# The split operands of the down projection, in longer tiles and at 28 different starting words

## The chip, the core and the metric

The kernel runs on one NeuronCore of one Trainium2 chip. A core has five engines that run side by side, each with its own instruction stream: TensorE (PE, with its weight loads shown apart as PEld), VectorE (DVE), ScalarE (ACT), GpSimd (POOL) and SyncE (SP), which here only issues DMAs. They work on SBUF, an on-chip memory of 128 partitions, and TensorE writes its sums into PSUM, a second memory. The metric is the time of one execution on the device in microseconds; of the kernel before there are three runs, and their median counts.

## The reference

One decoder block in float32 on `x` of 1 x 1024 x 1024: a pooling mixer and a sliding-window attention are merged through sigmoid gates and added to `x`, and then comes the MLP, on whose second half this case turns:

```
    h2 = _rmsnorm(x, g_mlp_pre[l])
    ff = jnp.einsum('bsf,fd->bsd',
                    jnp.square(jax.nn.relu(jnp.einsum('bsd,df->bsf', h2, w_up[l]))), w_down[l])
    x = x + _rmsnorm(ff, g_mlp_post[l])
```

`w_up` is 1024 x 4096 and `w_down` 4096 x 1024. The second product, of the squared activations (1024 x 4096) and `w_down`, is the down projection.

## The kernel before

**Products in split float32.** Every large product is made of three matmuls in the type float32r (`F32R`). A float32 operand is split by `split` into `hi` (a cast on ACT, line 101) and `lo` = source minus `hi` (a subtraction on DVE, line 104), and the product is the sum hi x hi + hi x lo + lo x hi, which is what the table `PASSES` lists.

**Seven products in place of eight.** The gates, the up projection and the down projection each cut both matrices in 2 x 2 blocks and use seven block products of sums and differences of blocks (a Strassen-like scheme). For the down projection the up projection has stored the needed sums of its activations in `f_dram`; the differences of the blocks B11, B12, B21, B22 of `w_dn` are made on DVE in `operands` (lines 1245 to 1259).

**The down projection (to line 1360).** The seven products run in the order `PRODUCTS = (1, 5, 2, 3, 6, 7, 4)`. Each has `NS` = 8 steps, so there are 56 steps `(i, s_)` in one list. A step covers 256 rows of the contraction. `operands(i, s_)` brings a step's two source tiles by DMA (lines 1222, 1227 and 1236), makes the difference of weights where one is needed, and splits both: the activations `ft` into two tiles of the pool `wp`, tag "wh" (six slots), the weights `wt` into two tiles of the pool `ga_`, tag "ga" (six slots too). Then `down_mm` issues the 24 matmuls of the step: two blocks of 128 rows, four tiles `t` of 128 output rows, three passes. The activations are the stationary operand, loaded anew for each matmul (128 x 128); the weights are the moving operand, 512 columns.

Everything is written out in the order in which it is issued: at step `j` stands first `operands` of step `j + AHEAD` with `AHEAD` = 2, then the matmuls of step `j`. Six slots of two tiles a step hold the operands of three steps. The operands of step (1, 0) are made earlier, during the up projection, in other tiles (lines 1181 to 1190); the loop and the line before it call `operands` for the other 55 steps. Each product adds up in four PSUM tiles, tag "at" or "mm"; at its end these are copied or added into SBUF tiles. The last three steps of the last product (i = 4) are taken tile by tile: 18 matmuls finish one `t`, and then DVE and ACT do that tile's closing work (lines 1276 to 1346) while TensorE does the next.

**Where the tiles lie.** A tile has the same byte address in each partition. The slots of "wh" and "ga" are 4096 bytes long (2 x 512 float32). In the program as built, every slot that holds an operand of a large matmul, in these pools and in the others, begins 32 bytes past a multiple of 64, and within a slot the matmuls' operands begin at multiples of 512 bytes.

Of the kernel before, what the change touches and what calls it, by code (L numbers as in the profile page):

```python
# [9 lines left out]
F32R = mybir.dt.float32r  # L10
# [4 lines left out]
P = 128  # L15
# [35 lines left out]
def block_kernel(ctx: ExitStack, tc, xt, x, consts, vecs, sinks, b_qkv, g_post, g_mlp, g_mlp_post,  # L51
# [7 lines left out]
    wp = ctx.enter_context(tc.tile_pool(name="wp", bufs=6))  # L59
# [8 lines left out]
    def nm(s):  # L68
        cnt[0] += 1
        return f"{s}_{cnt[0]}"  # L70
# [4 lines left out]
    def wslot(shape):  # L75
        return wp.tile([P] + shape, F32R, tag="wh", name=nm("wh"))
# [3 lines left out]
    ga_ = ctx.enter_context(tc.tile_pool(name="ga", bufs=6))  # L80
# [18 lines left out]
    def split(hi, lo, src, eng=dve, first=None):  # L99
        if first is None:  # L100
            act.copy(hi, src)  # L101
        else:
            first.tensor_copy(hi, src)
        eng.tensor_tensor(lo, src, f32(hi), ALU.subtract)  # L104
# [435 lines left out]
    def ar(shape):  # L540
        return ga_.tile([P] + shape, F32R, tag="ga", name=nm("ar"))
# [268 lines left out]
    def gr(shape):  # L810
        return gp.tile([P] + shape, F32R, tag="g", name=nm("gr"))
# [61 lines left out]
    for p in range(8):  # L873
# [8 lines left out]
        tag = "at" if p % 2 == 0 else "mm"  # L882
# [248 lines left out]
    def f_block(c, s_):  # L1131
        return f_rows[s_, c]
# [41 lines left out]
    for p in range(1, NP):  # L1174
# [3 lines left out]
        tag = "at" if p % 2 == 0 else "mm"  # L1178
        if p == NP - 1:
# [6 lines left out]
            fo = wslot([2, 512]), wslot([2, 512])  # L1186
            split(*fo, early_raw[0][0])
            wo_ = gr([2, 512]), gr([2, 512])
# [23 lines left out]
    def raw_tile():  # L1212
        return dl.tile([P, 2, 512], F32, tag="raw", name=nm("raw"), bufs=4)
# [2 lines left out]
    rr = sp.tile([P, NT], F32, tag="frr", name="frr", bufs=1)  # L1216
    junk = dl.tile([P, 512], F32, tag="junk", name="junk", bufs=1)
    res, xf = {}, {}

    def resident(name, s_):  # L1220
        t = rp.tile([P, 2, 512], F32, tag="w", name=nm(name))
        nc.sync.dma_start(t, w_block(name, s_))
        res[name, s_] = t

    def streamed(name, s_):
        t = raw_tile()
        nc.sync.dma_start(t, w_block(name, s_))
        return t

    def operands(i, s_):  # L1230

        if i == 1 and s_ in early_raw:
            ft, wt = early_raw[s_]
        else:
            ft = raw_tile()
            nc.sync.dma_start(ft, f_block(A_OF[i], s_))
            if i == 1:
                resident("B11", s_)
                if s_ - 3 in early_raw:
                    resident("B11", s_ - 3)  # L1240
                wt = res["B11", s_]
            elif i == 5:
                resident("B12", s_)
                wt = res["B11", s_]
                dve.tensor_tensor(wt, res["B12", s_], wt, ALU.subtract)
            elif i == 2:
                wt = streamed("B21", s_)
            elif i == 3:
                resident("B22", s_)
                wt = res["B22", s_]  # L1250
            elif i == 6:
                wt = res["B11", s_]
                dve.tensor_tensor(wt, res["B22", s_], wt, ALU.subtract)
            elif i == 7:
                wt = res["B12", s_]
                dve.tensor_tensor(wt, res["B22", s_], wt, ALU.subtract)
            else:
                wt = streamed("B21", s_)
                dve.tensor_tensor(wt, wt, res["B11", s_], ALU.subtract)
        fo = wslot([2, 512]), wslot([2, 512])  # L1260
        split(*fo, ft)
        wo_ = ar([2, 512]), ar([2, 512])
        split(*wo_, wt)
        opers[i, s_] = fo, wo_

# [43 lines left out]
    for j in range(1, AHEAD):  # L1309
        operands(*steps[j])  # L1310
    for j, (i, s_) in enumerate(steps):
        if j + AHEAD < len(steps):
            operands(*steps[j + AHEAD])
        if s_ == 0 and i not in (2, 3):
            tag = "mm" if i in (5, 7) else "at"
# [117 lines left out]
```

## Time and profile before

| what | us |
|---|---|
| median of three runs (lowest, highest) | 1133.97 (1133.69, 1134.46) |
| the profiled execution, its own time | 1134.51 |
| its span in the profile | 1132.7 |
| PE busy in the span | 1114.8 (98%), 5183 matmuls |
| PE weight loads busy | 920.9 (81%) |
| DVE busy | 820.6 (72%) |
| ACT busy | 526.7 (47%) |
| POOL busy | 77.8 (7%) |

The span goes from the first to the last instruction of the program; 1.8 us of the profiled execution lie around it. A group's row gives line, engine, operation, the tiles it writes and reads (out<-in, buffer numbers left out), shapes and count, then busy time, the mean length of one in ns, and the idle time before them with what ended it. The chain is the work that ended last, followed back from the last instruction; its rows give start, length and what it was. A matmul's row is longer than its turn on TensorE, because matmuls overlap: how fast they follow each other is read from the chain, where a row's length divided by its count is the turn of one. The down projection is line 1270.

### The profile page before, as it was taken

The numbers are of one execution on the slowest core, as the hardware profiler recorded it, in microseconds if no ns is written. First come the engines' busy times: TensorE is split into PE (matmuls) and PEld (weight loads), VectorE is DVE, ScalarE is ACT, GpSimd is POOL, SyncE is SP. The second block draws the span as 40 slices with busy tenths as digits, with TensorE's granted clock in tenths as the row PEclk, the third lists the DMA queues.
The fourth block names the chain that finished last, engine by engine and source line by source line (L and its number), as shares of the span: only waits on it lengthen the run. The fifth ranks groups of instructions, "written<-read, shape, count | busy, mean of one in ns | idle before, by whom it ended". The sixth has DMA issues, their size and how long they took to land.

```text
span 1132.7 us, 14023 instructions
## 1 busy us (share of the span) xinstructions
PE 1114.8 (98%) x5183; PEld 920.9 (81%) x5183; DVE 820.6 (72%) x1210; ACT 526.7 (47%) x912; POOL 77.8 (7%) x111
## 2 busy tenths in 40 slices
PE   8999999999999999999999999999999999999997
PEld 7888778888888888888788888888888888888885
DVE  7668857899858885678998666666457955446787
ACT  6445655544432333446555444444444345344342
POOL 2443211000000330000000000000000000000000
PEclk9999999999999999999999999999999999999999
DMA  7205669366664444243365343434597765332652
GB/s 248 84 1 110 151 138 285 117 224 220 211 236 141 143 158 154 94 149 112 121 230 202 145 160 141 164 139 167 214 337 266 242 203 189 110 93 75 215 192 94
DMA packets 80179, 189.02 MB, mean 167 GB/s; under 512 B 6896, under 2 KB 19312, under 8 KB 80112
## 3 DMA queue, kind: packets, MB, share of 16 engines
q1 hardware_dynamic: 70144, 166.38, 43.8%
q10 hardware_dynamic: 5616, 19.66, 4.5%
q0 software_dynamic: 4352, 2.10, 1.8%
q8 instruction: 40, 0.66, 0.2%
q14 instruction: 27, 0.22, 0.1%
HBM read 132.54 MB, written 55.57 MB: 166 GB/s over the span
## 4 chain that ended last, share of the span: by engine, by line
PE 87%; DVE 7%; ACT 3%; DMA 2%; issue 1%; SPq 0%; DVEq 0%; ACTq 0%
PE mm L484 22%; PE at L484 16%; PE at L1270 14%; PE mm L1270 12%; PE mm L987 6%; PE mm L421 5%; PE mm L183 3%; PE mm L423 3%; PE mm L574 2%; PE at L987 1%; PE at L192 1%; DVE wh L104 1%; PE at L392 1%; PE sc L328 1%; DMA st<-in_w_up_dram 1%
## 5 line engine op out<-in xcount | busy, mean ns | idle before, releaser
L1270 PE MATMUL at<-ar,wh 128*128 128x512 f32 x744 | 169.6, 389 | 0.0
L1270 PEld LDWEIGHTS at<-ar,wh 128*128 128x128 f32 x744 | 139.6, 188 | 29.3 <-DVE ar L104 0.4
L1270 PE MATMUL mm<-ar,wh 128*128 128x512 f32 x576 | 131.0, 389 | 0.0
L1270 PEld LDWEIGHTS mm<-ar,wh 128*128 128x128 f32 x576 | 108.1, 188 | 22.5
L104 DVE TENSOR_TENSOR wh<-raw,wh 128x1024 fp32r<-128x1024 f32 x53 | 64.8, 1223 | 83.4 <-ACT wh L101 83.4
L101 ACT CAST wh<-raw 128x1024 fp32r<-128x1024 f32 x53 | 55.8, 1053 | 133.9 <-PE at L1270 60.3
L101 ACT CAST wh<-st 128x512 fp32r<-128x512 f32 (+1 forms) x105 | 66.3, 642 | 84.6 <-PE at L484 29.9
L104 DVE TENSOR_TENSOR wh<-st,wh 128x512 fp32r<-128x512 f32 (+1 forms) x105 | 81.8, 789 | 29.6 <-ACT wh L101 27.1
L484 PE MATMUL mm<-gr,wh 128*128 128x512 f32 x309 | 74.2, 390 | 0.0
L484 PE MATMUL mm<-T,wx 128*128 128x512 f32 x288 | 67.6, 389 | 0.0
L484 PEld LDWEIGHTS mm<-gr,wh 128*128 128x128 f32 x309 | 57.8, 188 | 11.8
L484 PEld LDWEIGHTS mm<-T,wx 128*128 128x128 f32 x288 | 54.1, 188 | 11.2
L484 PE MATMUL at<-T,wx 128*128 128x512 f32 x252 | 59.1, 389 | 0.0
L484 PEld LDWEIGHTS at<-T,wx 128*128 128x128 f32 x252 | 47.3, 188 | 9.8
L484 PE MATMUL mm<-x,wh 128*128 128x512 f32 x240 | 55.2, 389 | 0.0
L484 PEld LDWEIGHTS mm<-x,wh 128*128 128x128 f32 x240 | 45.1, 188 | 9.3
L104 DVE TENSOR_TENSOR ar<-B,ar 128x1024 fp32r<-128x1024 f32 x37 | 45.1, 1219 | 6.6 <-ACT ar L101 6.4
L574 PE MATMUL mm<-x,wh 128*128 128x512 f32 x192 | 47.6, 396 | 0.0
L101 ACT CAST ar<-B 128x1024 fp32r<-128x1024 f32 x37 | 38.9, 1050 | 8.8 <-DMA B<-in_w_dn_dram 6.0
L484 PE MATMUL at<-gr,wh 128*128 128x512 f32 x174 | 42.3, 390 | 0.0
L574 PEld LDWEIGHTS mm<-x,wh 128*128 128x128 f32 x192 | 35.2, 188 | 7.8
L484 PEld LDWEIGHTS at<-gr,wh 128*128 128x128 f32 x174 | 32.6, 188 | 7.2 <-DVE gr L104 0.5
(362 smaller groups left out, 2188.3 us busy)
## 6 DMA issues: line engine op xcount, KB each, us to landing
raw<-f_dram SPq DMA_DIRECT2D x53, 512.0 KB, 3.8
f_dram<-g SPq DMA_DIRECT2D x30, 512.0 KB, 3.3
B<-in_w_dn_dram SPq DMA_DIRECT2D x24, 512.0 KB, 6.6
st<-in_w_up_dram SPq DMA_DIRECT2D x22, 512.0 KB, 3.7
st<-in_w_g_dram SPq DMA_DIRECT2D x18, 512.0 KB, 4.2
f_dram<-g ACTq DMA_DIRECT2D x17, 512.0 KB, 2.6
g<-spill_dram SPq DMA_DIRECT2D x16, 512.0 KB, 4.4
raw<-in_w_dn_dram SPq DMA_DIRECT2D x16, 512.0 KB, 4.6
```

The lines of the kernel that those rows point to most:

```text
L101: act.copy(hi, src)
L104: eng.tensor_tensor(lo, src, f32(hi), ALU.subtract)
L183: pe.matmul(bq, xs_[k][n // 4][:, xh, n % 4 * P:(n % 4 + 1) * P], wq[k][:, h, :], start=k == 0 and j == 0, stop=k == NK - 1 and j == 2)
L192: pe.matmul(bkv_of(n), xs_[k][n // 4][:, xh, n % 4 * P:(n % 4 + 1) * P], wkv[k // 2][:, h, k % 2, :], start=k == 0 and j == 0 and not (joi ...
L328: pe.matmul(sb[:, kv, i, :nk], qt[r, qx, m * P:(m + 1) * P], kx[r, k0:k0 + nk], start=j == 0, stop=j == 2)
L392: pe.matmul(flat(yb), v[:, kv, :], flat(p[:, 4 * kv:4 * kv + 4]), start=j == 0, stop=j == len(mms) - 1)
L421: pe.matmul(bs[th], whi[:, k, :], rhs(k, hl, th), start=k == 0 and hl == 0, stop=False)
L423: pe.matmul(bs[th], wlo[:, k, :], rhs(k, 0, th), start=False, stop=k == nk - 1)
L484: pe.matmul(b, w[:, wh, kt, :], xo[kt][:, xh, :], start=not after and kt == 0 and j == 0, stop=kt == 3 and j == 2, skip_group_check=after)
L574: pe.matmul(b, (whi, wlo)[h][:, k, :], xr(k, xh, th), start=j == 0, stop=j == len(mms) - 1)
L987: pe.matmul(obs[n][dj], l, wos[k][whl][:, dj * 512:(dj + 1) * 512], start=k == 0 and hl == 0 and whl == 0, stop=k == NK - 1 and hl == 1)
L1270: pe.matmul(bs[t], fo[fh][:, k2, t * P:(t + 1) * P], wo_[wh][:, k2, :], start=not after and s2 == 0 and k2 == 0 and j == 0, stop=s2 == NS ...
```

## The change

The tiles for the split operands of the down projection are no longer `[P, 2, 512]` but `[P, 1040]`, that is 4160 bytes, and the 1024 values lie in them from word `o` on (a word is one float32, 4 bytes). `a` is the starting word of both activation tiles of a step (stationary), `b` that of both weight tiles (moving). Two steps that follow each other share one entry of `OFFSETS`; the entries are first the 16 combinations of 0, 4, 8 and 12, then twelve others. 55 steps take 27 entries twice and the last entry, (8, 9), once.

```diff
+    placed = []
+
+    WORDS = (0, 4, 8, 12)
+    OFFSETS = [(a, b) for a in WORDS for b in WORDS] + [
+        (0, 1), (1, 0), (1, 1), (0, 2), (2, 0), (2, 2), (0, 15), (15, 0), (15, 15), (8, 10), (10, 8), (8, 9)]
+
+    def apart(tp, tag, o):
+
+        t = tp.tile([P, 1040], F32R, tag=tag, name=nm("op"))
+        return t[:, o:o + 1024].rearrange("p (a b) -> p a b", b=512)
...
-        fo = wslot([2, 512]), wslot([2, 512])
+        a, b = OFFSETS[len(placed) // 2]
+        placed.append((i, s_))
+        fo = [apart(wp, "wh", a) for _ in range(2)]
         split(*fo, ft)
-        wo_ = ar([2, 512]), ar([2, 512])
+        wo_ = [apart(ga_, "ga", b) for _ in range(2)]
         split(*wo_, wt)
         opers[i, s_] = fo, wo_
```

A slot of a tag is as long as its longest tile, so all slots of "wh" and "ga" become 4160 bytes, for the whole kernel. In the program as built, the pools that lie behind them (`sp`, `ga`, and the tiles `ap`, `gp`, `dl`) move by 384 or 768 bytes; all slots still begin 32 bytes past a multiple of 64. The instructions of each of the five engines stand in the same order as before, with the same shapes and the same waits; only the tile names (`op`) and the addresses differ. Other tiles of the tags "wh" and "ga", used by the earlier stages, begin at their slot's first byte as before.

## The prediction

> **What bounds the kernel now.** I read the page first, then the chain that ended last over the down projection, then the groups of line 1270, and then the timeline of one step. The page says that TensorE has work nearly all the time, at full clock:
>
> ```profile
> span 1132.7 us, 14023 instructions
> PE 1114.8 (98%) x5183; PEld 920.9 (81%) x5183; DVE 820.6 (72%) x1210; ACT 526.7 (47%) x912; POOL 77.8 (7%) x111
> PEclk9999999999999999999999999999999999999999
> ```
>
> The chain shows how the matmuls follow each other. Five of its rows from the down projection, then the closing work of the four last tiles:
>
> ```profile
> 820.61 43.52 PE at L1270 x192
> 864.13 43.52 PE mm L1270 x192
> ...
> 1038.21 43.52 PE mm L1270 x192
> 1081.73 31.99 PE at L1270 x140
> 1113.74 0.70 DVE u L1346
> ...
> 1117.80 0.61 DVE u L1346
> ...
> 1128.28 0.75 DVE xf L1300
> ```
>
> Each product of 192 matmuls takes 43.52 us: 226.7 ns a matmul, 5.44 us a step of 24, one product starting in the very place where the other ends. Nothing else stands in the chain from 820.61 to 1113.74. In the groups, TensorE is never idle before these matmuls:
>
> ```profile
> L1270 PE MATMUL at<-ar,wh 128*128 128x512 f32 x744 | 169.6, 389 | 0.0
> L1270 PE MATMUL mm<-ar,wh 128*128 128x512 f32 x576 | 131.0, 389 | 0.0
> ```
>
> These 744 + 576 = 1320 matmuls are the ones whose operands the change moves (55 steps of 24). So the question is one number: does a matmul still take its turn of 226.7 ns when its operands begin at other words? Every nanosecond more or less per matmul is up to 1.32 us of the end.
>
> **The change part by part.** *Longer slots, moved pools.* Instructions, order and waits are those of before: 0 us for them. The addresses of other stages' tiles move by multiples of 64 bytes. That the pace could depend on which slot a tile lies in, the trace lets me exclude: the up projection works on tiles of other pools,
>
> ```profile
> 556.75 13.60 PE mm L484 x60
> ...
> 630.21 19.04 PE at L484 x84
> ```
>
> and 19.04/84 and 13.60/60 are 226.7 ns again. Cost 0.
>
> *The engines that write the operands.* ACT and DVE now write, and DVE reads back, from odd words. For DVE the trace has such work: the pooling adds a row to itself shifted by one word (line 659), beside the subtraction of the split:
>
> ```profile
> L104 DVE TENSOR_TENSOR wh<-raw,wh 128x1024 fp32r<-128x1024 f32 x53 | 64.8, 1223 | 83.4 <-ACT wh L101 83.4
> L659 DVE TENSOR_TENSOR t<-d 128x1023 f32<-128x1023 f32 x4 | 4.9, 1225 | 3.7 <-ACT d L655 3.7
> ```
>
> 1225 ns against 1223: a word's shift costs DVE nothing. ACT has no such row with a wide tile. Its ends are nothing and, as a far bound, a cast of twice the length. What hides it is the lead of the operands:
>
> ```profile
> 929.22 1.05 ACT L101 CAST wh<-raw 128x1024 fp32r<-128x1024 f32 x1 [3.43 <-PE at L1270]
> 930.17 1.05 ACT L101 CAST ar<-raw 128x1024 fp32r<-128x1024 f32 x1
> 930.30 1.22 DVE L104 TENSOR_TENSOR wh<-raw,wh 128x1024 fp32r<-128x1024 f32 x1 [3.08 <-ACT wh L101]
> 931.44 1.22 DVE L104 TENSOR_TENSOR ar<-raw,ar 128x1024 fp32r<-128x1024 f32 x1
> 934.66 1.05 ACT L101 CAST wh<-raw 128x1024 fp32r<-128x1024 f32 x1 [3.43 <-PE at L1270]
> ```
>
> The casts begin when TensorE frees the slots of a step, 929.22, and the operands are whole at 931.44 + 1.22 = 932.66. They are for two steps later, 929.22 + 2 x 5.44 = 940.1: 7.4 us of lead. Casts of twice the length take 2.1 us of it, and 4.2 us of ACT's 5.44 us a step. I take 0 with both ends hidden.
>
> *The stationary operand, word `a`.* A weight load that begins at a word does stand in the trace: line 406 loads columns 0 to 7 of a tile, one float32 apart, repeated over 128 columns; line 371 loads whole tiles.
>
> ```profile
> L406 PEld LDWEIGHTS mm<-cst,r x8: 134/136/137, 65.1 to 66.5; 128*128 128x128 f32 x8
> L371 PEld LDWEIGHTS at<-cst,s x64: 138/140/143, 76.2 to 168.1; 128*128 128x128 f32 x64
> 76.55 0.87 PE at L371 x8
> ```
>
> 136 ns against 140: no cost, though these are reads of one repeated word and so only near the case. There is room besides: in the third row eight loads with short matmuls follow each other every 0.87/8 = 109 ns, so a load fits twice into a turn of 226.7 ns (218). The ends are 0 and, from twice the load on, the part that sticks out. I take 0.
>
> *The moving operand, word `b`.* This is what no row shows: every moving operand of a wide matmul begins at the same place within 64 bytes. What lies below nothing is a fixed part of a turn that placement might cause. The chain has the same kind of matmul with half the columns:
>
> ```profile
> 50.08 2.87 PE at L192 x24
> L202 PE MATMUL mm<-zeros x11: 393/628/792, 1.5 to 5.5; 128*128 128x512 f32 x11
> ```
>
> 2.87/24 = 119.6 ns for 256 columns and 226.7 for 512 leave 2 x 119.6 - 226.7 = 12.5 ns that don't go with the columns. So the low end is -12.5 ns a matmul. The high end is the second row, the longest I find for this shape: a median of 628 ns instead of 389, +239 ns, about a doubled turn. Between -12.5 and +239 I take 0, since it is nearest to all the rows with wide matmuls, which keep 226.7 ns across pools, stages, tags and columns within a slot.
>
> [...]
>
> *Sum.* 0 + 0 + 0 + 0 = 0. Against the profiled execution that is its own 1134.51 us (span 1132.7 and 1.8 around it), which lies 0.54 above the median of the runs; the forecast for the median is thus 1134.0. What a measurement can tell from no change is about 0.2%, 2.3 us.
>
> **The rivals.** *Odd words slow the moving stream (slower).* If words are fetched in pairs, a stream from an odd word has its pairs across a border. Odd `b` have (0,1), (1,1), (0,15), (15,15) with 48 matmuls each and (8,9) with 24: 216. It decides from 2.3 us/216 = 10.6 ns a matmul. A fully doubled turn gives 216 x 226.7 = 49.0 us, 1183; half of that, pairs broken half the time, 24.5 us, 1158.5. For it: nothing in the trace excludes it. Against: DVE's shifted row, on another engine.
>
> *Every start away from the present one costs a piece (slower).* If the stream is fetched in blocks of 64 bytes and a different start touches one more, that is 16 of 512 columns, an estimated 7.1 ns. `b` is not 0 in 12 of the first 16 entries (576 matmuls) and in 9 of the other twelve, one of them half (408): 984 x 7.1 = 7.0 us, 1141. Against it: the present start, 32 bytes past a border, already touches one block more than the least. It decides from 2.3 ns.
>
> *The present placement costs the 12.5 ns (faster).* The stationary and the moving operand of every matmul now begin at the same place within 64 bytes. If their reads collide for that reason, entries with `a` different from `b` would lose the fixed part: 12 of the first 16 and 9 of the others, again 984 matmuls, 12.3 us. The last 72 matmuls gain little: four closings of DVE and ACT follow each other every 4.1 us (1113.74 to 1117.80), as long as 18 matmuls, so 0.9 us stays. That is -11.4 us, 1122.6; with half of the collisions gone 1128.3. For it: the fixed part exists, equal everywhere, as is the placement. Against: an equal price everywhere fits a price of changing weights just as well. [...]
>
> **How the numbers follow.** No effect, within 0.2%: 0.52, time 1134.0, own range 1133 to 1136. Odd words slow: 0.20. Every other start slow: 0.14. Collisions gone: 0.14. So faster 0.14, same 0.52, slower 0.34. The range reaches down to 1126 (all of the collision case but its strong half) and up to 1158 (the whole of the second case and the weaker half of the first): 0.52 + 0.07 + 0.14 + 0.10 = 0.83.
>
> **What the changed profile would show.** If I am right, the chain has seven pieces of line 1282 (1270 before) at 43.52 us for 192 matmuls, DVE's and ACT's rows stay at 1.22 and 1.05 us, and no wait of TensorE appears. The places tell the cases apart. Step `j` starts at 820.61 + 5.44 j, and entry p serves steps 2p + 1 and 2p + 2: odd words can only show from step 33, 1000.1 us on, in the last three products, in (0,1) and (1,1) and not in their neighbours (1,0) and (0,2). A cost of every other start, or a collision that ends, shows from step 3 on, within the first product, as a piece other than 43.52. The forecast is wrong if turns other than 226.7 ns stand in any entry; a weight load that matters would show in (1,0), (2,0) and (15,0) alone.

## The result

The changed kernel takes 1148.68 us (median of four runs, 1147.63 to 1149.97), the kernel before 1133.83 us. The ratio is 1.0133 with a 95% interval of 1.0118 to 1.0148: 14.8 us slower, clearly more than the 2.3 us that count as a change, and inside the range on record (1126 to 1158).

The page of the changed kernel: the same instructions, a granted TensorE clock of 0.996 as before, 14.2 us more span, and 16.2 us more in which PE is busy.

```profile
span 1146.9 us, 14023 instructions
PE 1131.0 (99%) x5183; PEld 921.6 (80%) x5183; DVE 821.4 (72%) x1210; ACT 527.2 (46%) x912; POOL 77.8 (7%) x111
PEclk9999999999999999999999999999999999999999
```

The chain that ended last, from the end of the up projection on (start, length, what, count):

```profile
654.11 19.34 PE mm L484 x84
673.44 19.34 PE at L484 x84
692.78 19.16 PE mm L484 x84
...
827.61 44.41 PE at L1282 x192
872.02 44.41 PE mm L1282 x192
916.43 44.60 PE at L1282 x192
961.03 44.56 PE mm L1282 x192
1005.59 44.97 PE at L1282 x192
1050.56 44.49 PE mm L1282 x192
1095.04 44.75 PE at L1282 x192
1139.79 0.02 issue
1139.81 0.70 DVE u L1358
```

The down projection (line 1282 now) begins at 827.61 us, where it began at 820.61: half of the loss, 7.0 us, is there before the first matmul that the edit names. The up projection's pieces of 84 matmuls take 19.16 to 19.34 us instead of 19.04 (228.1 to 230.2 ns a matmul, not 226.7). The gates ahead of it lose as well; their first long piece, in the kernel before and in the changed one:

```profile
178.23 43.52 PE mm L484 x192
```

```profile
177.66 44.28 PE mm L484 x192
```

The other half lies in the down projection, whose products take 44.4 to 45.0 us instead of 43.52. The first of them, with the entries (0,0) to (0,12), is already 0.9 us longer; the longest, the fifth at 44.97 us, holds the odd words (0,1) and (1,1) and exceeds the others by 0.2 to 0.6 us only. TensorE still waits for nothing, and the engines that write the operands work at their old pace (before, 1223 ns a subtraction and 1053 a cast of the activations):

```profile
L1282 PE MATMUL at<-op,op 128*128 128x512 f32 x744 | 173.8, 395 | 0.0
L104 DVE TENSOR_TENSOR op<-raw,op 128x1024 fp32r<-128x1024 f32 x69 | 83.4, 1225 | 91.8 <-ACT op L101 91.8
L101 ACT CAST op<-raw 128x1024 fp32r<-128x1024 f32 x69 | 71.3, 1049 | 148.3 <-PE at L1282 69.6
```

So the matmuls' turns got longer, by 4.0 ns in the piece of the gates, by 1.4 to 3.5 ns in the pieces of the up projection and by 4.6 to 7.6 ns in the products of the down projection, and no wait was added.

### The profile page after: what moved, and what is told of

It reads as the page before. It is cut to its first block, busy times and chain, and to the rows that moved or that the text cites. A ratio compares the mean times of both kernels' runs of the same rounds, so it can differ in the third digit from the quotient of the medians.

```text
span 1146.9 us, 14023 instructions
## 1 busy us (share of the span) xinstructions
PE 1131.0 (99%) x5183; PEld 921.6 (80%) x5183; DVE 821.4 (72%) x1210; ACT 527.2 (46%) x912; POOL 77.8 (7%) x111
## 3 DMA queue, kind: packets, MB, share of 16 engines
q0 software_dynamic: 4352, 2.10, 1.8%
## 4 chain that ended last, share of the span: by engine, by line
PE 90%; DVE 6%; ACT 2%; DMA 1%; issue 1%; DVEq 0%; ACTq 0%
PE mm L484 22%; PE at L484 16%; PE at L1282 16%; PE mm L1282 12%; PE mm L987 7%; PE mm L421 5%; PE mm L183 3%; PE mm L423 3%; PE mm L574 2%; PE at L987 1%; PE at L192 1%; PE at L392 1%; PE sc L328 1%; DVE wh L104 1%; PE sc L183 1%
## 5 line engine op out<-in xcount | busy, mean ns | idle before, releaser
L1282 PE MATMUL at<-op,op 128*128 128x512 f32 x744 | 173.8, 395 | 0.0
L1282 PEld LDWEIGHTS at<-op,op 128*128 128x128 f32 x744 | 139.8, 188 | 33.3 <-DVE op L104 0.3
L104 DVE TENSOR_TENSOR op<-raw,op 128x1024 fp32r<-128x1024 f32 x69 | 83.4, 1225 | 91.8 <-ACT op L101 91.8
L101 ACT CAST op<-raw 128x1024 fp32r<-128x1024 f32 x69 | 71.3, 1049 | 148.3 <-PE at L1282 69.6
L1282 PE MATMUL mm<-op,op 128*128 128x512 f32 x576 | 133.9, 394 | 0.0
L1282 PEld LDWEIGHTS mm<-op,op 128*128 128x128 f32 x576 | 108.3, 188 | 25.1
L104 DVE TENSOR_TENSOR op<-B,op 128x1024 fp32r<-128x1024 f32 x37 | 45.2, 1221 | 6.8 <-ACT op L101 6.6
L101 ACT CAST op<-B 128x1024 fp32r<-128x1024 f32 x37 | 38.7, 1046 | 8.9 <-DMA B<-in_w_dn_dram 6.2
```

The costliest lines, as they stand in the source:

```text
L1282: pe.matmul(bs[t], fo[fh][:, k2, t * P:(t + 1) * P], wo_[wh][:, k2, :], start=not after and s2 == 0 and k2 == 0 and j == 0, stop=s2 == NS ...
```

## The experiments

What had to be told apart is which part of the edit does this: the slots of 4160 bytes, the starting words, or the mere move of the pools. The idea that came from the changed profile, called theory A in the expectations: in the kernel before all slots begin at the same place within 256 bytes (in the program as built, 224 bytes past a multiple of 256), because 4096 is a multiple of 256. With steps of 4160 bytes the slots lie at four places, 64 bytes apart. All kernels below are the changed kernel with the edit shown; "turn" is the mean distance from one matmul's start to the next.

**The longer slots without the words.**

```diff
-    OFFSETS = [(a, b) for a in WORDS ...
+    OFFSETS = [(0, 0)] * 28
```

> Slots of 4160 bytes as in the change, but every operand at word 0. Theory A (places within 256 bytes): a turn is 226.7 ns only where the stationary and the moving operands that follow each other all begin at the same place within 256 bytes; slots that step by 4160 bytes spread the places, and the words add little. Expected: the down projection starts at 827 to 828 us as in the changed kernel (820.6 before), its products take 44.2 to 44.8 us (43.52 before), the time is 1144 to 1149. Theory B (words): the words alone made the down projection slower, the longer slots only the stages ahead of it. Expected: products of 43.5 us and 1140 to 1142.

Measured: 1148.97 us, ratio 1.0127 (1.0109 to 1.0145). Its chain:

```profile
814.83 14.14 PE mm L484 x62
828.97 44.45 PE at L1280 x192
...
1006.89 44.46 PE at L1280 x192
```

The words may be left away altogether and the time of the changed kernel stays. The down projection begins a microsecond later than theory A expected; its products and the time are as expected. Theory B is out.

**Still longer slots, at the old place.**

```diff
+    OFFSETS = [(0, 0)] * 28
-        t = tp.tile([P, 1040], F32R, tag=tag, name=nm("op"))
+        t = tp.tile([P, 1088], F32R, tag=tag, name=nm("op"))
```

> Slots of 4352 bytes, which is 17 times 256, and every operand at word 0: the slots are longer still and the pools behind them move by 1536 and 3072 bytes, but each tile begins at its old place within 256 bytes. Theory A: 226.7 ns everywhere, products of 43.52 us, 1133.5 to 1134.5. Theory C (any longer slot or moved pool costs, whatever the place): 1145 to 1150.

Measured: 1133.25 us, ratio 0.9992 (0.9982 to 1.0001). The products are back:

```profile
820.02 43.52 PE at L1280 x192
863.54 43.52 PE mm L1280 x192
```

Slots that are longer by 256 bytes, and pools moved by up to 3072, cost nothing. It is the place within 256 bytes, not the length or the move as such. In the change both displace tiles: the slots step by 4160 bytes, and the pool `ga` moves by 384 bytes, the growth of the six slots ahead of it, which is 128 beyond a multiple of 256. The steps alone suffice in the first piece of the gates, whose operands lie in "wh" and in the tiles `x`, in a pool that isn't among those that move: it takes 44.28 us in the change and with longer slots without the words, 43.52 before and in this run. What the move of `ga` adds elsewhere, no run separates.

**The words alone.** The same slots of 4352 bytes, with the 28 entries of the change.

> Slots of 4352 bytes with the 28 pairs of words of the change. Theory A: everything ahead of the down projection is as before (start at 820.6), and in it the pairs of steps show their words alone. If only the place of stationary against moving counts, (0,0), (4,4), (8,8), (12,12), (1,1), (2,2) and (15,15) have 226.7 ns and the others 228 to 237; if the place itself counts, only (0,0) has. All together 3 to 7 us more than before, 1137 to 1141. Theory B: the words cost all of the down projection's share in the change, 7 us, and the two halves of the table differ: 1141. Under both the odd word 1 of the moving operand costs most (about 237 ns) and the odd word 15 nothing, as in the changed kernel.

Measured: 1139.82 us, ratio 1.0052 (1.0036 to 1.0068). Now each entry stands on even ground, and its turn can be read: the chain in the stretches of (0,0), (0,8), (4,0), (12,8), (0,1) and (0,15), in this order, each with 48 or 49 matmuls.

```profile
824.01 11.11 PE at L1282 x49
846.00 11.20 PE at L1282 x48
868.40 11.20 PE mm L1282 x48
979.36 11.11 PE mm L1282 x49
1001.28 11.38 PE at L1282 x48
1068.58 11.14 PE mm L1282 x49
```

That is 226.7 ns for (0,0), 233.3 for (0,8) and (4,0), 226.7 for (12,8), 237.1 for (0,1) and 227.3 for (0,15). The words cost 5.9 us by themselves, as theory A expected (3 to 7); the slots of the change (15.0 us by themselves) hide this: with both, it is 14.8. Its simple form, that only the place of stationary against moving counts, fell, though. Equal words were not always fast (233.3 ns in (4,4), 237.4 in (1,1), against 226.7 in (8,8)), and some unequal ones were.

**A map of the moving word.**

```diff
+    OFFSETS = [(0, b) for b in range(0, 64, 4)] + [(16, 0), (32, 0), (48, 0), (16, 16), (32, 32), (48, 48), (8, 8),
+               (0, 1), (0, 3), (0, 15), (1, 1), (0, 0)]
```

> Slots of 4352 bytes; the pairs of steps take moving words 0, 4, 8 ... 60 with the stationary at 0, then stationary words 16, 32, 48 with the moving at 0, then both at 16, 32, 48 and 8, then moving words 1, 3, 15, both at 1, and both at 0. Theory A: 226.7 ns at (0,0), and again where both have moved by the same, with 228 to 236 ns between, in a course that depends on the difference within 256 bytes; no course within 64 bytes alone, so words 16, 32 and 48 cost although they are whole multiples of 64 bytes. A rival (lines of 64 bytes): words 16, 32, 48 cost nothing, 226.7 ns, and the course of 0 to 12 repeats four times. A third (places of 16 bytes do not matter, chance rules): no course, all at 229 to 233 ns.

One run: 1139.81 us. The chain in the stretches of (0,0), (0,16), (0,32), (0,48), and of the second step of (16,16):

```profile
825.25 11.11 PE at L1280 x49
869.64 11.00 PE mm L1280 x48
914.03 11.38 PE at L1280 x49
958.82 11.19 PE mm L1280 x48
...
1042.41 5.21 PE mm L1280 x23
```

226.7, 229.2, 232.2 and 233.1 ns: words 16, 32 and 48, whole multiples of 64 bytes, cost too, so the line of 64 bytes is out, and so is chance. In (16,16), once it has settled, the turn is 226.5 ns; (32,32), (48,48) and (8,8) gave 226.6 to 227.0 in their second steps. The turns of (16,0), (32,0) and (48,0), from the first matmul's start to the last one's, are 233.2, 232.4 and 229.0; read the same way, (0,48), (0,32) and (0,16) have 233.2, 232.5 and 229.1. At multiples of 32 bytes it is thus the difference of the two starting places that counts. Of (0,4) to (0,56) no step is below 228.9 ns, but (0,60) is fast (below); the slowest multiple of 32 bytes is (0,40) with 234.3.

**One unequal pair for all steps.**

```diff
+    OFFSETS = [(0, 8)] * 28
```

> Slots of 4352 bytes, all 55 steps with the stationary operand at word 0 and the moving one at word 8. The price by steps, 233.4 instead of 226.7 ns, times 1320 matmuls is 8.8 us: 1142 to 1143, products of 44.8 us. If the price were one of changing places between steps rather than of the places themselves, it would be gone here: 1134.

Measured: 1141.82 us, ratio 1.0066 (1.0048 to 1.0084), 7.7 us by the medians where 8.8 were expected; the interval reaches from 5.4 to 9.5. The second to the sixth product have

```profile
864.86 44.80 PE mm L1280 x192
909.66 44.80 PE at L1280 x192
```

233.3 ns a matmul. The price belongs to the places, not to a change of places between steps.

**Both operands 64 bytes on, for all steps.** `OFFSETS = [(16, 16)] * 28`.

> Slots of 4352 bytes, all 55 steps with both operands at word 16, 64 bytes on. If only the place of one operand against the other counts (at multiples of 32 bytes), 226.7 ns and 1133 to 1134.5. If the old place itself, 32 bytes before a multiple of 256, is the good one, 229 to 233 ns and 1137 to 1142.

Measured: 1133.53 us, ratio 0.9996 (0.9987 to 1.0006); its products take 43.52 us from the second on. The old place is not better than this one; being at the same one is what counts.

**256 bytes apart.** `OFFSETS = [(0, 64)] * 28`.

> Slots of 4352 bytes, the stationary operand at word 0 and the moving one at word 64, 256 bytes on. If places count within 256 bytes, 226.7 ns, products of 43.52 us, 1132 to 1135. If the difference in bytes counts whatever its size, 231 to 233 ns, products of 44.4 to 44.8 us, 1140 to 1143.

One run: 1134.18 us beside 1132.98 for the kernel before on the same chip, and

```profile
820.22 43.52 PE at L1280 x192
863.74 43.52 PE mm L1280 x192
```

A difference of 256 bytes costs nothing here: 226.7 ns a matmul. With (0,16), (0,32) and (0,48) at 229.2, 232.2 and 233.1 ns, the course repeats after 256 bytes, as far as this one point shows it, and not after 64 or 128.

**One tag alone in longer slots.**

```diff
-        wo_ = [apart(ga_, "ga", b) for _ in range(2)]
+        wo_ = ar([2, 512]), ar([2, 512])
```

with tiles of 1040 words in "wh" and every word 0.

> Slots of 4160 bytes for the tag wh alone (the stationary operands of the down projection, and a part of the operands of the stages ahead of it), slots of 4096 bytes for ga, every operand at word 0. If the place of stationary against moving counts, spreading one tag spreads the differences nearly as well as spreading both: 1143 to 1149, products of 44.1 to 44.6 us. If each tag's spread costs its own part, about half: 1140 to 1142.

One run: 1149.05 us beside 1132.98; the down projection begins at 830.02, and its first products are

```profile
830.02 44.27 PE at L1280 x192
874.29 44.29 PE mm L1280 x192
```

Longer slots for one tag cost as much as for both (16.1 us in this one run, 15.0 by the medians there), as they should if the difference between the two counts. The other theory, a price for each tag of its own, is out.

**Does what came before matter?** In the two tables (12,8) and (0,60) were fast and (4,0) slow, though in each pair the stationary word is 4 ahead, modulo 64. Two runs with the entries in other orders.

```diff
+    OFFSETS.reverse()
```

> Slots of 4352 bytes, the 28 pairs of words of the change in reversed order. So far (4,8), (12,4) and (12,8) kept 226.7 ns, while (4,0), (4,4) and (8,0), with like differences, took 233.3. Theory M (memory): the turn depends on what came before too, since the matmuls fall into one of several rhythms and stay there; in reversed order some of these seven pairs change by 3 ns or more. Theory P (place alone): each pair keeps its turn within 1 ns of the run with the order of the change: (4,8) 226.7, (12,4) 226.7, (12,8) 226.7, (4,0) 233.3, (4,4) 233.3, (12,12) 230, (0,15) 227, (15,15) 228.3, (0,1) and (1,1) 237.

```diff
+    OFFSETS = [(0, 0), (4, 0), (0, 0), (12, 8), (0, 0), (12, 4), (0, 0), (4, 8), (0, 0), (4, 4), (0, 0), (12, 12),
+               (0, 0), (0, 60), (0, 0), (8, 0), (0, 0), (0, 8), (0, 0), (15, 15), (0, 0), (2, 2),
+               (0, 0), (0, 8), (4, 8), (0, 8), (12, 8), (0, 8)]
```

> Slots of 4352 bytes; each pair of words comes after a pair of steps at (0,0), which has 226.7 ns: (4,0), (12,8), (12,4), (4,8), (4,4), (12,12), (0,60), (8,0), (0,8), (15,15), (2,2); then (4,8) and (12,8) once more, each between two (0,8), which has 233.4 ns. Theory P: every pair has the turn of before: (4,0) 233.3, (12,8) 226.7, (12,4) 226.7, (4,8) 226.7, (4,4) 233.3, (12,12) 230, (0,60) 227, (8,0) 233.3, (0,8) 233.4, (15,15) 228.3, (2,2) 231.2, and (4,8) and (12,8) have 226.7 after (0,8) too. Theory M: (4,0) and (4,4) keep about 227 when they come out of the fast rhythm, and (4,8) and (12,8) stay near 233 when they come out of the slow one.

One run each: 1139.57 and 1136.01 us. In reversed order the chain in the stretch of (12,8) is

```profile
969.49 10.97 PE mm L1283 x47
```

233.4 ns where it was 226.7. After (0,0), the stretches of (4,0) and (0,60):

```profile
835.13 10.88 PE at L1280 x48
966.71 11.19 PE mm L1280 x48
```

(4,0) has now 226.7 ns where it had 233.3, and (0,60) 233.1 where the map had

```profile
992.47 5.68 PE mm L1280 x25
998.15 5.21 PE at L1280 x23
```

227 ns. So theory P is out: the places alone don't fix the turn. The slots don't explain it either: (12,8) had 226.7 ns in step 30 and 233.3 in step 27 of the reversed order, which lie in the same product (i = 3) and, six slots being three steps, in the same slots. A memory, as theory M has it, is the likelier reading, though not in the way it said: (12,8) was slow after the fast (0,0). For it speaks that (0,4) and (0,12), with the same entries ahead of them in the run of the words and in that of the map, had the same turns in both, 231.6 and 233.2 ns, while (0,12) had 230.0 in the reversed order. It isn't shown, since each order was profiled once, and a choice that differs from one execution to the next would look alike. By more than 1 ns it touches, among the entries that can be compared, only pairs with an operand 16 bytes off a multiple of 32 (one more is (4,4), 233.3, 231.1 and 230.0 in the three orders). (0,0), (8,8), (0,8) and (8,0) kept their turns within 0.5 ns once settled, whatever stood ahead, and so did the odd words (1,1), 237.2 to 237.8, and (0,15), 227.0 to 227.3.

**One tile of the four displaced.** `wo_ = [apart(ga_, "ga", o) for o in (0, 8)]` moves the lo tile of the weights alone, `fo = [apart(wp, "wh", o) for o in (0, 8)]` the lo tile of the activations alone.

> Slots of 4352 bytes; only the lo tile of the moving weights begins at word 8, all else at word 0. Of the three matmuls of a group (hi hi, hi lo, lo hi; stationary first) only the second has unequal places. If the price belongs to a matmul with unequal places, a third of it: 226.7 + 6.7/3 = 228.9 ns, products of 43.95 us, 1136 to 1138. If any change of the moving place from matmul to matmul costs (two of three turns), about 231 ns, 1139 to 1141.

> Slots of 4352 bytes; only the lo tile of the stationary activations begins at word 8, all else at word 0. Only the third matmul of a group has unequal places; its weights are loaded while the second runs. If the price belongs to one unequal pair, whether the load against the stream ahead or a matmul's own two operands, 228.9 ns, products of 43.95 us, 1136 to 1138, as with the moving lo tile. If each change of place costs anew, about 231 ns, 1139 to 1141.

One run each: 1139.80 and 1141.52 us beside 1132.98. The products, of the first and then of the second kernel:

```profile
863.90 44.48 PE mm L1280 x192
```

```profile
863.69 44.80 PE mm L1280 x192
```

231.7 and 233.3 ns. Both expectations of a third of the price failed: one displaced tile of four, unequal in one matmul of three, costs 5.0 and 6.6 of the 6.7 ns. The other branch, a price for each change of place, fits the first kernel (about 231 ns, 1139 to 1141) and not the second, and the run with (0,8) in all steps has the price with no such change at all. With the stationary lo tile displaced the starts follow each other at 233, 239 and 228 ns, over and over, a sum of 700; in the kernel with equal places it is 227, 227, 226, a sum of 680. The unequal matmul is the third, with 228. The longest turn is that of the second, and in the trace the load of the displaced weights begins 2 ns after the second matmul and takes 188 ns. So most of the price, 12 of 20 ns, falls where these weights are loaded beside a stream from another place; the 6 ns in the first turn stay unexplained.

## Why the prediction was right or wrong

The time lies in the range, but that is luck: no effect, 1134.0 us, was the likeliest case, and the range reached to 1148.68 only for the sake of slower rivals, of which none named what happened. By its own sign the forecast was wrong: the first product, with the entries (0,0) to (0,12), already took 231.3 ns a matmul and not 226.7.

**The bound** was right: TensorE bounds the down projection, nothing else enters the chain from 827.61 to 1139.79 us, and the longer turn is paid in the time: with (0,8) in all steps 6.7 ns on 1320 matmuls make 8.8 us, and the medians show 7.7 (5.4 to 9.5). 44.80 instead of 43.52 us a product in the run with (0,8) is the turn of 233.3 ns and nothing besides. (The chain there shows four rows of the down projection, not five.)

**"Longer slots, moved pools ... Cost 0" is the step that failed.** It is worth 15.0 us alone, as much as the whole change (14.8). I had excluded it with rows of other stages whose tiles lie in other pools and have the same 226.7 ns. Those rows show that the slot does not matter only as long as all slots begin at one place within 256 bytes, and in that kernel all did; with slots of 4160 bytes the up projection's rows have 228.1 to 230.2 ns. I had seen the addresses, 32 bytes past a multiple of 64 for every slot, and read "moved by multiples of 64 bytes" as "not moved". The rows had no variety in the very thing that the change varies. The same error made me look for the price in the down projection alone, while half of it came in the stages ahead, which share the slots.

**The writers.** Right: DVE's subtractions take 1225 ns and ACT's casts 1049, and no wait of TensorE appears.

**The stationary word** was costed at 0 because a load fits twice into a turn. Wrong: (8,0), (16,0) and (32,0) take 233.3, 233.2 and 232.4 ns, and the sign named for it, a cost in (1,0), (2,0) and (15,0), shows on even ground with 232.3, 230.6 and 230.0. The load is hidden as an occupation of time (188 ns of a turn of 226.7, and TensorE is not idle before these matmuls); the place of its operand against the moving one still counts in the turn. Line 406, one repeated word, was too far from the case.

**The moving word** was taken as 0 between -12.5 and +239 ns. The turn is not independent of the two places: the moving word costs up to 7.6 ns at multiples of 32 bytes (234.3 ns in (0,40)) and 10 at word 1 (237.1 in (0,1)). The words of both operands together cost 5.9 us with slots on even ground; in the change itself, on its uneven slots, they add nothing that the runs show (14.8 us with them, 15.0 without).

**The rivals.** "Every start away from the present one costs a piece" came nearest, with 7.1 ns a matmul where (0,8) has 6.7; but its reason, one more block of 64 bytes, is wrong, since (16,16) to (48,48) cost nothing (226.5 to 227.0 ns) and (0,16) costs (229.2). "Odd words" was far oversized: 10 ns at word 1 and 0.3 to 0.6 at word 15, not 113 to 227. "The present placement costs the 12.5 ns" had the sign wrong: equal places at multiples of 32 bytes are among the best found, and no unequal pair is faster. In no run does the mean of any 24 matmuls that follow each other in the down projection fall below 226.6 ns.

What stays open is the reason underneath. The runs show turns (226.7 ns at differences of 0 and 256 bytes, 229.2 to 233.1 at 64, 128 and 192), not why they differ. Why pairs 16 bytes off have more than one rhythm ((12,8): 226.7 and 233.4 ns), and why word 1 costs 10 ns and word 15 next to nothing (0.3 to 0.6 ns), is not settled either.

## What to carry to other kernels

Where matmuls follow each other without a gap, try to let all tiles that they read begin at the same place within 256 bytes, and at a multiple of 32 bytes. In this kernel the turn was 226.7 ns there and 229 to 234 at differences of other multiples of 32 bytes, and equal places off these were slow ((4,4) 230.0 to 233.3 ns, (1,1) 237). Slots of 4352 bytes, a multiple of 256, kept the time (1133.25 us), slots of 4160 did not (1148.97). A pad of 64 bytes on two tags cost 1.3% here, half of it in stages that the edit never mentioned. And before excluding an effect by rows that agree, check that these rows differ in the thing that the change varies.

## What the runs showed of the hardware that was not expected

- A float32r matmul of 512 columns with its weight load took 226.7 ns from start to start when both operands began at the same place within 256 bytes, a multiple of 32 bytes (226.5 to 227.0 in the pairs measured), and 229 to 233 ns at 64, 128 and 192 bytes of difference (16, 32, 48 words: 229.2, 232.2, 233.1). At 256 bytes of difference (64 words) it was 226.7 again.
- A stationary operand displaced by 32 bytes in one matmul of three lengthened the turns of the other two as well, most of all of the one ahead: 227, 227 and 226 ns became 233, 239 and 228.
- With an operand 16 bytes off a multiple of 32 the same pair of words had different steady turns in different orders of the entries: (12,8), (4,0) and (0,60) each showed about 227 and about 233 ns. That the work ahead decides is likely, not shown.
- A moving operand from word 1, with the stationary one at word 0, cost 10 ns a matmul (237.1 ns), from word 15 0.3 to 0.6 (227.0 to 227.3). The DVE subtraction took 1225 ns with the operands at the change's words, 1223 without.
